# First stage of a two-block transformer kernel: the first gate row summed on GpSimd, the softplus chain moved to GpSimd

## The chip, the cores and the metric

The kernel runs on one core of one Trainium2 chip. Its engines are TensorE (PE in the profile, PEld for its weight loads), VectorE (DVE), ScalarE (ACT), GpSimd (POOL) and SyncE (SP), which here only issues DMAs. The metric is the device time of one execution in microseconds; the median of several runs is compared.

## What is computed

Two blocks run one after the other on 256 positions of width 1024, all in float32. The first block has two layers whose shifts, scales and gates are computed from a condition vector `c`. The part that matters here is the first half of its first layer, the RG-LRU mixer:

```python
c_act = jax.nn.silu(c)
mod = (c_act @ ada_w[i] + ada_b[i])[:, None, :]
sh_m, sc_m, gt_m, sh_f, sc_f, gt_f = jnp.split(mod, 6, axis=-1)
h = rmsnorm(x, norm_g[i, 0]) * (1.0 + sc_m) + sh_m
y = rglru_mixer(h, ...)          # first layer
x = x + gt_m * rmsnorm(y, norm_g[i, 1])
```

Inside the mixer, `log_a = -8 * r * softplus(-lam)` needs the softplus of one vector of 1024 values, and `r` and a second gate come from small block-diagonal products. After that come a scan along the positions, a GeLU gate branch of full width and the output projection. The row `gt_m * norm_g[0, 1]` is the gate row: 1024 values, the same for all positions, needed only when the output of the mixer is added to `x`. Everything behind that (the feed-forward part, the second layer, the second block of four layers) is the rest of the program, by far the most of the time, and the change does not touch it.

## The kernel before

The program is straight-line code, written with a framework that places the waits and picks the order of instructions on each engine: it follows the order of the program, but puts an instruction forward where the one ahead is not yet ready by its own reckoning. A DMA or an instruction that is pinned (`keep_in_program_order`) stays behind everything that was written before it on its engine. At run time each engine, and SP's queue of DMAs, works strictly in the order that was fixed. Tiles of one name share a fixed number of buffers (`bufs`); a load into a buffer waits on SP until the last reader of the buffer is done, and what stands behind it on SP waits too.

The weights come as chunks of 128x1024 (512 KB), tile `raw`, four buffers. Most are split into a high and a low half: ACT rounds the high half (line 369), VectorE subtracts it (line 370), and every product is made of three fast passes (lines 432 to 434 and 439 to 441) that read high and low halves.

The first stage runs as follows.

- `ada_init` loads `c` into all partitions and makes `cact`, twice the SiLU of `c`, in all partitions.
- `rg_x` (lines 552 to 589) normalises `x`, transposes it, and also transposes `cact` into `crep`: chunk `kk` of `crep` holds in row p the value of `cact` at position 128 kk + p, 128 times side by side. Then, for each of eight chunks, VectorE computes two entries per partition of shift and scale (line 503: a row of `ada` times `cact`, summed along the row; the loads go into `adar` or `adag`, two buffers each), ACT makes the modulated tile, and PE adds the products with the first weights (line 588) in eight PSUM banks.
- `rg` computes the softplus chain on VectorE (lines 794 to 812, tiles of 128x8 called `lam`): a polynomial in z. Then the convolution over four positions (ACT line 814, VectorE line 816), and a loop over four groups with the small gate products (PE line 833), tanh and exponentials on ACT (lines 836 to 847) and three products on VectorE (lines 845, 846, 849). After it come the scan (lines 857, 859) and eight chunks of the gate branch (`up`, lines 439 to 441; GeLU, line 867; line 868; the split of the result, lines 444 and 445). In between, `bg` puts further rows of `ada` for later stages into VectorE's stream (line 503 again, pinned).
- `gate0` is a generator that is advanced twice in each of the four groups. Each step loads 128 rows of the gate's weights (`adag`, 128x1024, line 604, pinned on SP) and multiplies them on PE with `crep[:, kk, :]` as the stationary matrix (line 606): all 128 output rows are the same sum over the 128 partitions, added up over the eight steps in two PSUM banks of tag `y`. Its end adds twice the bias with a one-row matmul (line 609) and writes `row0`, half the sum times the norm's weight (line 610).
- `out_proj` (lines 432 to 434) multiplies the result with the output weights, position half 0 first, then half 1. `turn` takes a finished half, multiplies it with the gate row (line 647), normalises (GpSimd lines 525, 416, 417 compute the reciprocal root for 128 rows), adds it to `x` and prepares the next stage's input.

PSUM has eight banks here, four of tag `y` and four of tag `u`. GpSimd has only the reciprocal roots and a few fills.

Of the kernel before, what the change touches and what calls it, by code (L numbers as in the profile page):

```python
# [8 lines left out]
F32 = mybir.dt.float32  # L9
# [458 lines left out]
class Block1:  # L468
# [84 lines left out]
    def rg_x(self):  # L553
# [12 lines left out]
        self.crep = self.R.tile([128, 8, 128], F32, name="crep", tag="crep", bufs=1)  # L566
        for q in range(0, 8, 4):
            p = k.bank("u", 4, (128, 4, 128))
            for j in range(4):
                nc.tensor.transpose(p[:, j, :], self.cact[:, (q + j) * 128:(q + j + 1) * 128], k.ident)  # L570
            self.ACT.copy(out=self.crep[:, q:q + 4, :], in_=p)
# [19 lines left out]
    def gate0(self):  # L591

        k, Q, R, nc = self.k, self.Q, self.R, self.nc
        two = R.tile([1, 128], F32, name="two", tag="two", bufs=1)
        self.V.memset(two, 2.0)
        b = Q.tile([1, D], F32, name="gb0", tag="xn", bufs=2)
        k.tc.keep_in_program_order(nc.sync.dma_start(out=b, in_=self.a["gateb"][0:1]))
        self.row0 = Q.tile([128, D], F32, name="grow", tag="grow", bufs=1)
        k.tc.keep_in_program_order(nc.sync.dma_start(out=self.row0, in_=self.a["gateb"][1].partition_broadcast(128)))
        p = [k.bank("y", 4) for _ in range(2)]  # L600
        half = [slice(n * 512, n * 512 + 512) for n in range(2)]
        for kk in range(8):
            w = R.tile([128, D], F32, name="adag", tag="adag", bufs=2)
            k.tc.keep_in_program_order(nc.sync.dma_start(out=w, in_=self.a["adag"][kk]))
            for n in range(2):
                nc.tensor.matmul(p[n], self.crep[:, kk, :], w[:, half[n]], start=kk == 0, stop=False)
            yield
        for n in range(2):
            nc.tensor.matmul(p[n], two, b[:, half[n]], start=False, stop=True)
            self.V.scalar_tensor_tensor(out=self.row0[:, half[n]], in0=p[n], scalar=0.5, in1=self.row0[:, half[n]], op0=OP.mult, op1=OP.mult)  # L610

    def gate_row(self, i, w):

        if (i, w) == (0, 0):
            return self.row0
# [169 lines left out]
    def rg(self):  # L785
        k, R, V, ACT = self.k, self.R, self.V, self.ACT
        x, ub = self.rg_x()
        n2 = lambda nm, w=512, b=2, dt=F32: R.tile([128, w], dt, name=nm, tag=f"r_{nm}", bufs=b)

        lam = self.col("rg_lambda", 0, 8)  # L790
        ab, e, z, sp = (k.small(f"lam{q}", 8) for q in range(4))
        ACT.activation(out=ab, in_=lam, func=AF.Abs)
        ACT.activation(out=e, in_=ab, func=AF.Exp, scale=-1.0)
        V.tensor_scalar(out=z, in0=e, scalar1=2.0, scalar2=None, op0=OP.add)
        V.reciprocal(out=z, in_=z)
        V.tensor_tensor(out=z, in0=z, in1=e, op=OP.mult)
        z2, acc = k.small("lam4", 8), k.small("lam5", 8)
        V.tensor_tensor(out=z2, in0=z, in1=z, op=OP.mult)
        V.memset(acc, 2.0 / 19)
        for d in range(17, 0, -2):  # L800
            V.tensor_tensor(out=acc, in0=acc, in1=z2, op=OP.mult)
            V.tensor_scalar(out=acc, in0=acc, scalar1=2.0 / d, scalar2=None, op0=OP.add)
        V.tensor_tensor(out=acc, in0=acc, in1=z, op=OP.mult)
        V.tensor_scalar(out=sp, in0=lam, scalar1=-1.0, scalar2=0.0, op0=OP.mult, op1=OP.max)
        V.tensor_tensor(out=sp, in0=sp, in1=acc, op=OP.add)
        sp2, sp4 = k.small("sp2", 8), k.small("sp4", 8)
        V.tensor_scalar(out=sp2, in0=sp, scalar1=2.0, scalar2=None, op0=OP.mult)
        V.tensor_scalar(out=sp4, in0=sp, scalar1=-4.0, scalar2=None, op0=OP.mult)
        hb = k.small("hb", 16)
        V.tensor_scalar(out=hb, in0=self.col("rg_ba", 0, 16), scalar1=0.5, scalar2=None, op0=OP.mult)  # L810
# [742 lines left out]
```

## Time and profile before

| | |
|---|---|
| median of three runs | 2728.43 us (2728.37 to 2731.88) |
| the profiled execution | 2730.44 us, span 2728.6 us |
| PE busy | 2664.6 us, 98% of the span |
| DVE busy | 1905.7 us, 70% |
| ACT busy | 1410.7 us, 52% |
| POOL busy | 77.4 us, 3% |
| moved by DMA | 514.38 MB, mean 189 GB/s |

The span is from the first to the last instruction on the core; the execution's time is 1.8 us longer. The profile gives, for each engine, its instructions in order of time with the idle time ahead of each and what ended that idle time. Busy shares over the whole span say little about the first stage, which is short and mixes several limits; it is read from stretches of 10 us and from the order of time. An fp32 matmul appears as two records. One fp32 record of 512 columns takes some 0.44 us from start to start. PE's granted clock is full for nearly the whole span.

### The profile page before, as it was taken

The numbers are of one execution on the slowest core, as the hardware profiler recorded it, in microseconds if no ns is written. First come the engines' busy times: TensorE is split into PE (matmuls) and PEld (weight loads), VectorE is DVE, ScalarE is ACT, GpSimd is POOL, SyncE is SP. The second block draws the span as 40 slices with busy tenths as digits, with TensorE's granted clock in tenths as the row PEclk, the third lists the DMA queues.
The fourth block names the chain that finished last, engine by engine and source line by source line (L and its number), as shares of the span: only waits on it lengthen the run. The fifth ranks groups of instructions, "written<-read, shape, count | busy, mean of one in ns | idle before, by whom it ended". The sixth has DMA issues, their size and how long they took to land.

```text
span 2728.6 us, 44400 instructions
## 1 busy us (share of the span) xinstructions
PE 2664.6 (98%) x16744; PEld 2360.5 (87%) x16744; DVE 1905.7 (70%) x3780; ACT 1410.7 (52%) x2848; POOL 77.4 (3%) x115
## 2 busy tenths in 40 slices
PE   7899999999999999999999999999999999999998
PEld 5689877898899779989988899899889989977898
DVE  6889889877656776575565755756775575685755
ACT  4665654655444655444455544544754454455542
POOL 0000000000000000000000000000000000000000
PEclk9999999999999999999999999999999999999999
DMA  8868674665655537656654565664455565453652
GB/s 316 293 239 300 220 247 158 216 201 167 209 186 166 155 113 225 185 180 199 184 172 123 181 185 170 214 185 148 149 170 186 170 209 186 155 181 114 208 185 93
DMA packets 141080, 514.38 MB, mean 189 GB/s; under 512 B 16177, under 2 KB 16561, under 8 KB 139330
## 3 DMA queue, kind: packets, MB, share of 16 engines
q1 hardware_dynamic: 140866, 511.56, 57.9%
q8 instruction: 131, 2.15, 0.3%
q14 instruction: 83, 0.68, 0.1%
HBM read 510.44 MB, written 1.05 MB: 187 GB/s over the span
## 4 chain that ended last, share of the span: by engine, by line
PE 85%; issue 6%; DVE 4%; ACT 2%; DMA 1%; POOL 1%; DVEq 0%; POOLq 0%; SPq 0%; ACTq 0%
PE u L439 12%; PE u L440 12%; PE u L441 12%; PE y L434 11%; PE y L432 11%; PE y L433 11%; PE u L432 3%; PE u L433 3%; PE u L434 3%; DVE lo L370 2%; PE u L1234 2%; PE u L463 1%; DMA raw<-w 1%; PE u L1228 1%; PE u L1211 1%
## 5 line engine op out<-in xcount | busy, mean ns | idle before, releaser
L370 DVE TENSOR_TENSOR lo<-raw,hi 128x512 fp32r<-128x512 f32 (+4 forms) x1501 | 1081.4, 747 | 557.6 <-ACT hi L369 546.7
L369 ACT CAST hi<-raw 128x512 fp32r<-128x512 f32 (+4 forms) x1501 | 953.3, 667 | 796.4 <-issue 447.4
L439 PE MATMUL u<-hThi,hi 128*128 128x256 f32 x3016 | 855.2, 284 | 2.0 <-ACT hi L369 1.4
L441 PE MATMUL u<-hThi,lo 128*128 128x256 f32 x3016 | 852.6, 283 | 0.5 <-DVE lo L370 0.5
L440 PE MATMUL u<-hTlo,hi 128*128 128x256 f32 x3016 | 852.9, 283 | 0.0
L439 PEld LDWEIGHTS u<-hThi,hi 128*128 128x128 f32 x3016 | 576.9, 191 | 6.7 <-ACT hi L369 1.6
L440 PEld LDWEIGHTS u<-hTlo,hi 128*128 128x128 f32 x3016 | 577.2, 191 | 4.6 <-issue 1.0
L441 PEld LDWEIGHTS u<-hThi,lo 128*128 128x128 f32 x3016 | 576.9, 191 | 1.1 <-DVE lo L370 1.0
L432 PE MATMUL y<-hi,hT 128*128 128x512 f32 x704 | 278.9, 396 | 0.0
L433 PE MATMUL y<-lo,hT 128*128 128x512 f32 x704 | 278.3, 395 | 0.0
L434 PE MATMUL y<-hi,hT 128*128 128x512 f32 x704 | 278.2, 395 | 0.0
L432 PE MATMUL y<-hi,hThi 128*128 128x512 f32 (+6 forms) x504 | 192.1, 382 | 3.5 <-ACT hThi L444 3.3
L433 PE MATMUL y<-lo,hThi 128*128 128x512 f32 (+6 forms) x504 | 187.8, 373 | 0.1
L434 PE MATMUL y<-hi,hTlo 128*128 128x512 f32 (+6 forms) x504 | 186.4, 373 | 0.2 <-DVE hTlo L445 0.2
L434 PEld LDWEIGHTS y<-hi,hT 128*128 128x128 f32 x704 | 132.3, 188 | 31.9
L432 PEld LDWEIGHTS y<-hi,hT 128*128 128x128 f32 x704 | 132.4, 188 | 29.2
L433 PEld LDWEIGHTS y<-lo,hT 128*128 128x128 f32 x704 | 132.2, 188 | 28.9
L432 PE MATMUL u<-hi,hThi 128*128 128x512 f32 x320 | 127.5, 400 | 5.4 <-ACT hThi L444 5.4
L444 ACT CAST hT<-th 128x256 fp32r<-128x256 f32 x144 | 58.3, 405 | 130.2 <-DVE th L1100 130.2
L433 PE MATMUL u<-lo,hThi 128*128 128x512 f32 x320 | 125.6, 394 | 0.0
L434 PE MATMUL u<-hi,hTlo 128*128 128x512 f32 x320 | 123.3, 393 | 0.0
L432 PEld LDWEIGHTS y<-hi,hThi 128*128 128x128 f32 x504 | 96.3, 191 | 19.4 <-ACT hThi L444 5.2
(303 smaller groups left out, 3192.9 us busy)
## 6 DMA issues: line engine op xcount, KB each, us to landing
raw<-w SPq DMA_DIRECT2D x823, 512.0 KB, 3.7
adar<-ada SPq DMA_DIRECT2D x80, 512.0 KB, 4.8
gb<-lngb SPq DMA_DIRECT2D x12, 1024.0 KB, 4.6
adag<-ada SPq DMA_DIRECT2D x8, 512.0 KB, 5.8
adag<-adag SPq DMA_DIRECT2D x8, 512.0 KB, 4.5
raw<-w SPq DMA_DIRECT2D x8, 384.0 KB, 3.0
raw<-w SPq DMA_DIRECT2D x5, 480.0 KB, 3.5
raw<-w SPq DMA_DIRECT2D x4, 396.0 KB, 3.0
```

What stands on the lines that cost most here:

```text
L369: nc.scalar.copy(out=hi[:, a:b], in_=r[:, a:b])
L370: nc.vector.tensor_tensor(out=lo[:, a:b], in0=r[:, a:b], in1=hi[:, a:b].bitcast(F32), op=OP.subtract)
L432: mm(out, xhi, w[0], start=start, stop=False)
L433: mm(out, xhi, w[1], start=False, stop=False)
L434: mm(out, xlo, w[0], start=False, stop=stop)
L439: mm(out, whi, xhi, start=start, stop=False)
L440: mm(out, whi, xlo, start=False, stop=False)
L441: mm(out, wlo, xhi, start=False, stop=stop)
L444: self.nc.scalar.copy(out=hi, in_=src)
L463: self.nc.tensor.transpose(p[:, k * 128:k * 128 + 128], x[:, (h + k) * 128:(h + k + 1) * 128], self.ident)
L1211: nc.tensor.matmul(scores[e], qh(e), kh(e), start=True, stop=True)
L1234: nc.tensor.matmul(op[:, e, :], pTs[e // 2][:, e % 2, j, :], v[j][:, e, :], start=j == 0, stop=j == t)
```

## The change

The eight chunks of the gate's weights no longer go to PE. `crep` is replaced by `ccol`, one column per chunk (128x8 in all). GpSimd multiplies each chunk with its column and adds it to a sum tile `gsum` (128x1024); the first partition of the sum also takes twice the bias. The sum over partitions is then made by two fp32 matmuls with a matrix of ones, in `gate_row`, which is called after the output projection of half 0 has been written; their banks have tag `u`. The loads of bias, norm row and chunks are no longer pinned on SP. The softplus chain runs on GpSimd; the reciprocal becomes a power of -1 with an exponent tile.

```diff
--- before.py
+++ after.py
@@ -563,12 +563,12 @@
                     nc.tensor.transpose(p[:, q, t * 128:t * 128 + 128], xn[t][:, (kk + q) * 128:(kk + q + 1) * 128], k.ident)
             self.ACT.copy(out=xT[:, kk:kk + 2, :], in_=p)
 
-        self.crep = self.R.tile([128, 8, 128], F32, name="crep", tag="crep", bufs=1)
+        self.ccol = self.R.tile([128, 8], F32, name="ccol", tag="ccol", bufs=1)
         for q in range(0, 8, 4):
             p = k.bank("u", 4, (128, 4, 128))
             for j in range(4):
                 nc.tensor.transpose(p[:, j, :], self.cact[:, (q + j) * 128:(q + j + 1) * 128], k.ident)
-            self.ACT.copy(out=self.crep[:, q:q + 4, :], in_=p)
+            self.ACT.copy(out=self.ccol[:, q:q + 4], in_=p[:, :, 0])
         acc = [k.bank("y" if j < 4 else "u", 4) for j in range(8)]
         h = self.h_tiles()
         mod, dot = self.mod[0], self.dot[0]
@@ -591,27 +591,33 @@
     def gate0(self):
 
         k, Q, R, nc = self.k, self.Q, self.R, self.nc
-        two = R.tile([1, 128], F32, name="two", tag="two", bufs=1)
-        self.V.memset(two, 2.0)
+        G = nc.gpsimd
         b = Q.tile([1, D], F32, name="gb0", tag="xn", bufs=2)
-        k.tc.keep_in_program_order(nc.sync.dma_start(out=b, in_=self.a["gateb"][0:1]))
+        nc.sync.dma_start(out=b, in_=self.a["gateb"][0:1])
         self.row0 = Q.tile([128, D], F32, name="grow", tag="grow", bufs=1)
-        k.tc.keep_in_program_order(nc.sync.dma_start(out=self.row0, in_=self.a["gateb"][1].partition_broadcast(128)))
-        p = [k.bank("y", 4) for _ in range(2)]
-        half = [slice(n * 512, n * 512 + 512) for n in range(2)]
+        nc.sync.dma_start(out=self.row0, in_=self.a["gateb"][1].partition_broadcast(128))
+        s = self.gsum = R.tile([128, D], F32, name="gsum", tag="gsum", bufs=1)
         for kk in range(8):
             w = R.tile([128, D], F32, name="adag", tag="adag", bufs=2)
-            k.tc.keep_in_program_order(nc.sync.dma_start(out=w, in_=self.a["adag"][kk]))
+            nc.sync.dma_start(out=w, in_=self.a["adag"][kk])
+            c = self.ccol[:, kk:kk + 1]
+            if kk == 0:
+                G.tensor_scalar(out=s, in0=w, scalar1=c, scalar2=None, op0=OP.mult)
+                G.tensor_scalar(out=b, in0=b, scalar1=2.0, scalar2=None, op0=OP.mult)
+                G.tensor_tensor(out=s[0:1], in0=s[0:1], in1=b, op=OP.add)
+            else:
+                G.tensor_scalar(out=w, in0=w, scalar1=c, scalar2=None, op0=OP.mult)
+                G.tensor_tensor(out=s, in0=s, in1=w, op=OP.add)
+            yield
+
+    def gate_row(self, i, w):
+
+        if (i, w) == (0, 0):
             for n in range(2):
-                nc.tensor.matmul(p[n], self.crep[:, kk, :], w[:, half[n]], start=kk == 0, stop=False)
-            yield
-        for n in range(2):
-            nc.tensor.matmul(p[n], two, b[:, half[n]], start=False, stop=True)
-            self.V.scalar_tensor_tensor(out=self.row0[:, half[n]], in0=p[n], scalar=0.5, in1=self.row0[:, half[n]], op0=OP.mult, op1=OP.mult)
-
-    def gate_row(self, i, w):
-
-        if (i, w) == (0, 0):
+                h = slice(n * 512, n * 512 + 512)
+                p = self.k.bank("u", 4)
+                self.nc.tensor.matmul(p, self.ones, self.gsum[:, h], start=True, stop=True)
+                self.V.scalar_tensor_tensor(out=self.row0[:, h], in0=p, scalar=0.5, in1=self.row0[:, h], op0=OP.mult, op1=OP.mult)
             return self.row0
         k, Q = self.k, self.Q
         m = self.mods(i, 3 * w + 2)
@@ -785,29 +791,32 @@
     def rg(self):
         k, R, V, ACT = self.k, self.R, self.V, self.ACT
         x, ub = self.rg_x()
+        G = k.nc.gpsimd
         n2 = lambda nm, w=512, b=2, dt=F32: R.tile([128, w], dt, name=nm, tag=f"r_{nm}", bufs=b)
 
         lam = self.col("rg_lambda", 0, 8)
         ab, e, z, sp = (k.small(f"lam{q}", 8) for q in range(4))
+        self.inv = k.small("inv", 8)
+        G.memset(self.inv, -1.0)
         ACT.activation(out=ab, in_=lam, func=AF.Abs)
         ACT.activation(out=e, in_=ab, func=AF.Exp, scale=-1.0)
-        V.tensor_scalar(out=z, in0=e, scalar1=2.0, scalar2=None, op0=OP.add)
-        V.reciprocal(out=z, in_=z)
-        V.tensor_tensor(out=z, in0=z, in1=e, op=OP.mult)
+        G.tensor_scalar(out=z, in0=e, scalar1=2.0, scalar2=None, op0=OP.add)
+        G.tensor_tensor(out=z, in0=z, in1=self.inv, op=OP.pow)
+        G.tensor_tensor(out=z, in0=z, in1=e, op=OP.mult)
         z2, acc = k.small("lam4", 8), k.small("lam5", 8)
-        V.tensor_tensor(out=z2, in0=z, in1=z, op=OP.mult)
-        V.memset(acc, 2.0 / 19)
+        G.tensor_tensor(out=z2, in0=z, in1=z, op=OP.mult)
+        G.memset(acc, 2.0 / 19)
         for d in range(17, 0, -2):
-            V.tensor_tensor(out=acc, in0=acc, in1=z2, op=OP.mult)
-            V.tensor_scalar(out=acc, in0=acc, scalar1=2.0 / d, scalar2=None, op0=OP.add)
-        V.tensor_tensor(out=acc, in0=acc, in1=z, op=OP.mult)
-        V.tensor_scalar(out=sp, in0=lam, scalar1=-1.0, scalar2=0.0, op0=OP.mult, op1=OP.max)
-        V.tensor_tensor(out=sp, in0=sp, in1=acc, op=OP.add)
+            G.tensor_tensor(out=acc, in0=acc, in1=z2, op=OP.mult)
+            G.tensor_scalar(out=acc, in0=acc, scalar1=2.0 / d, scalar2=None, op0=OP.add)
+        G.tensor_tensor(out=acc, in0=acc, in1=z, op=OP.mult)
+        G.tensor_scalar(out=sp, in0=lam, scalar1=-1.0, scalar2=0.0, op0=OP.mult, op1=OP.max)
+        G.tensor_tensor(out=sp, in0=sp, in1=acc, op=OP.add)
         sp2, sp4 = k.small("sp2", 8), k.small("sp4", 8)
-        V.tensor_scalar(out=sp2, in0=sp, scalar1=2.0, scalar2=None, op0=OP.mult)
-        V.tensor_scalar(out=sp4, in0=sp, scalar1=-4.0, scalar2=None, op0=OP.mult)
+        G.tensor_scalar(out=sp2, in0=sp, scalar1=2.0, scalar2=None, op0=OP.mult)
+        G.tensor_scalar(out=sp4, in0=sp, scalar1=-4.0, scalar2=None, op0=OP.mult)
         hb = k.small("hb", 16)
-        V.tensor_scalar(out=hb, in0=self.col("rg_ba", 0, 16), scalar1=0.5, scalar2=None, op0=OP.mult)
+        G.tensor_scalar(out=hb, in0=self.col("rg_ba", 0, 16), scalar1=0.5, scalar2=None, op0=OP.mult)
         xc = R.tile([128, 8, 256], F32, name="xc", tag="big0", bufs=1)
         for j in range(8):
             u = ub[j]
```

## Rows read from the trace of the kernel before

**Rows 1.** The page, part 1: busy us (share of the span) and instructions.

```profile
PE 2664.6 (98%) x16744; PEld 2360.5 (87%) x16744; DVE 1905.7 (70%) x3780; ACT 1410.7 (52%) x2848; POOL 77.4 (3%) x115
```

**Rows 2.** Stretches: length, then busy us and instructions per engine, PE clock, DMA.

```profile
70.00:80.00 10.00, 4.80 (x16) 3.09 (x16) 6.64 (x11) 8.56 (x16) 0.00 (x0) 0.87 0.87 313
80.00:90.00 10.00, 10.00 (x66) 8.29 (x65) 10.00 (x16) 8.04 (x11) 0.00 (x0) 0.95 0.93 342
```

**Rows 3.** PE in order: start, us, line, tiles, count, [idle before <-releaser].

```profile
50.66 3.66 PE L606 MATMUL y<-adag,crep 128*128 128x512 f32 x8
...
58.84 3.60 PE L606 MATMUL y<-adag,crep 128*128 128x512 f32 x8
...
78.00 2.93 PE L606 MATMUL y<-adag,crep 128*128 128x512 f32 x3 [5.20 <-DMA adag<-adag]
...
82.56 0.69 PE L439 MATMUL u<-hThi,hi 128*128 128x256 f32 x1
...
94.15 1.98 PE L609 MATMUL y<-gb,two 1*128 1x512 f32 x4
...
```

**Rows 4.** VectorE in order of time, 48 to 96 us.

```profile
53.19 4.75 DVE L816 SCALAR_TENSOR_TENSOR xc<-u,cols,xc 128x255 f32<-128x255 f32 x12
...
67.27 0.69 DVE L849 SCALAR_TENSOR_TENSOR xc<-wx,xc 128x512 f32<-128x512 f32 x1 [2.71 <-ACT wx L836]
...
76.70 1.23 DVE L503 SCALAR_TENSOR_TENSOR adar<-adar,cact 128x1024 f32<-128x1024 f32 x1 [3.32 <-DMA adar<-ada]
...
79.06 1.22 DVE L370 TENSOR_TENSOR lo<-raw,hi 128x1024 fp32r<-128x1024 f32 x1
...
94.58 1.21 DVE L370 TENSOR_TENSOR lo<-raw,hi 128x1024 fp32r<-128x1024 f32 x1
```

**Rows 5.** ACT in order of time, at 63 us.

```profile
63.45 0.63 ACT L847 ACTIVATE d<-d 128x512 f32<-128x512 f32 x1 [2.62 <-DVE wa L846]
```

**Rows 6.** VectorE and PE in order of time, 114 to 135 us.

```profile
119.21 1.23 DVE L370 TENSOR_TENSOR lo<-raw,hi 128x1024 fp32r<-128x1024 f32 x1 [0.40 <-ACT hi L369]
...
122.92 0.68 DVE L647 TENSOR_TENSOR yg<-y,grow 128x512 f32<-128x512 f32 x1
...
119.23 0.50 PE L432 MATMUL y<-hi,xchi 128*128 128x512 f32 x1 [0.41 <-ACT hi L369]
...
128.42 0.50 PE L433 MATMUL y<-lo,xchi 128*128 128x512 f32 x1 [0.76 <-DVE lo L370]
```

**Rows 7.** GpSimd's groups by shape: count | busy us, mean ns | idle before.

```profile
L525 POOL TENSOR_SCALAR mss<-ss 128x1 f32<-128x1 f32 x14 | 11.3, 808 | 539.4 <-ACT pj L646 504.6 <-ACT pj L654 22.8 <-DVE mod L514 12.0
...
L925 POOL MEMSET AT<- 128x1024 f32 x1 | 1.0, 951 | 3.6 <-PE y L434 3.6
L925 POOL MEMSET AT<- 128x512 f32 x1 | 0.5, 521 | 0.0
...
L416 POOL TENSOR_SCALAR ms<-ss 128x1 f32<-128x1 f32 x2 | 0.4, 190 | 5.1 <-ACT junk L536 5.1
```

**Rows 8.** GpSimd in order of time, at 342 us.

```profile
342.35 2.43 POOL L525 TENSOR_SCALAR mss<-ss 128x1 f32<-128x1 f32 x1
```

**Rows 9.** VectorE in order of time beside it.

```profile
342.20 1.21 DVE L370 TENSOR_TENSOR lo<-raw,hi 128x1024 fp32r<-128x1024 f32 x1
343.33 1.28 DVE L445 TENSOR_TENSOR hTlo<-hf,hThi 128x512 fp32r<-128x512 f32 x2
344.53 1.28 DVE L647 TENSOR_TENSOR yg<-y,grow 128x512 f32<-128x512 f32 x2
```

**Rows 10.** SP's queue in order of time: start, us, line, load, count.

```profile
44.66 1.67 SPq L604 DMA_DIRECT2D adag<-adag  x2
...
71.48 6.81 SPq L501 DMA_DIRECT2D adar<-ada  x2
```

**Rows 11.** The tile adag: time from a load's issue to its landing.

```profile
DMA to landing us min/median/max: 3.4/5.7/9.2
```

**Rows 12.** ACT in order of time, at 17 us.

```profile
17.36 0.60 ACT L548 ACTIVATE hf<-xnT,mod,A 128x256 f32<-128x256 f32 x1 [0.48 <-DVE lam L801]
```

More of the change, by code (lines that the diff above doesn't have):

```diff
@@ L607, in gate0 @@
             yield
-        for n in range(2):
-            nc.tensor.matmul(p[n], two, b[:, half[n]], start=False, stop=True)
-            self.V.scalar_tensor_tensor(out=self.row0[:, half[n]], in0=p[n], scalar=0.5, in1=self.row0[:, half[n]], op0=OP.mult, op1=OP.mult)
     def gate_row(self, i, w):
         if (i, w) == (0, 0):
+            for n in range(2):
+                h = slice(n * 512, n * 512 + 512)
+                p = self.k.bank("u", 4)
+                self.nc.tensor.matmul(p, self.ones, self.gsum[:, h], start=True, stop=True)
+                self.V.scalar_tensor_tensor(out=self.row0[:, h], in0=p, scalar=0.5, in1=self.row0[:, h], op0=OP.mult, op1=OP.mult)
```

## The prediction

> **What bounds the kernel now.** I read the page's engine shares first: PE is busy for 98% of the span [rows 1], so a microsecond that PE loses or wins in the first stage stays in the time to the end. Then the busy time in stretches of 10 us, because the change touches only the first 135 us: there the picture is another one. From 80 us on VectorE is busy for the whole of each stretch, and in 70 to 80 us PE stands still for half [rows 2]. Third, the instructions of each engine in order of time, to see which one waits for which.
>
> PE's timeline shows what the removed matmuls cost where they stand [rows 3]. The 16 fp32 matmuls appear as 32 records of line 606, eight of them in 3.6 us, so some 14 us in all; the two small ones of line 609, four records, take 2.0 us. But PE has to wait anyway. The first eight (from 50.66 us) lie beside the convolution of VectorE. The second eight (58.84 to 62.3 us) lie before products whose reader, ACT, is held: its row at 63.45 us waits for VectorE's line 846, and the tanh of those products comes only behind it [rows 5]. The third group begins with 5.20 us of waiting for a weight, and the gate branch's products start behind it at 82.56 us. They need the low half of a weight that VectorE begins at 79.06 and ends near 80.3 us. The last group ends at 96.1 us, just when VectorE has the next low half ready (94.58 + 1.21 = 95.8 us) [rows 4].
>
> So VectorE sets the pace from 60 to 119 us. Its gaps there are 2.71 us at 67.27 and 3.32 us at 76.70 us, 6.0 us together [rows 4]; after 76.70 us there is none of note until 119.21 us [rows 6].
>
> **The change part by part.**
>
> *TensorE's matmuls go.* By the above the first, second and last blocks are covered by VectorE or ACT. Of the third, PE could begin the gate products near 80.3 instead of 82.6 us, but it would only meet VectorE's next low halves sooner. I cost this edit at nothing. What hides it is VectorE's work; if VectorE came earlier, the removal would begin to pay.
>
> *The softplus chain moves to GpSimd.* 29 small VectorE instructions leave the first 25 us. Ahead of the first modulated tile they cost a little: ACT's row at 17.36 us waits 0.48 us, last for one of them [rows 12]. I take -0.5 us, between 0 (the weights of the next step are awaited anyway) and -1.0, twice that wait. On GpSimd the chain has until the gate tanhs behind the convolution, and is hidden there.
>
> *Eight weighted sums come to GpSimd.* No row shows GpSimd on a tile of that size with an input, so I bound it. Writing 128x1024 takes 0.95 us and 128x512 0.52 us, 0.84 ns per column; a one-column tensor-scalar takes 0.19 us [rows 7]. A one-input instruction is then 0.19 + 1024 x 0.84 ns = 1.05 us (estimate). The two-input add lies between one pass, 1.05 us, and three passes (two reads, one write), 2.75 us; I take two, 1.9 us, since only its second input is new against the one-input row. A chunk is then 2.95 us, between 2.1 and 3.8. [...]
>
> When does it run? The first chunk's DMA is issued at 44.66 us, when VectorE has released the buffer [rows 10], and lands 5.7 us later by the median [rows 11]: 50.4 us. Chunk 0 with the bias row (1.05 + 1.9) ends at 53.3, chunk 1 at 56.3, chunk 2 near 60 us. Until 57.9 us VectorE runs the convolution, whose first input is in PSUM [rows 4]. Five chunks are left, 14.75 us (10.5 to 19).
>
> Do they run beside VectorE? The trace has a row for that. GpSimd's one-column sum at 342.35 us takes 2.43 us and ends only after VectorE's two-input subtractions, which run until 344.61 us; the next VectorE row, with one input in PSUM, does not hold it [rows 8, 9]. The 14 sums of that line average 0.81 us, although a one-column tensor-scalar can take 0.19 us [rows 7]. So a GpSimd instruction that reads SBUF makes no progress while VectorE reads two SBUF operands, which nearly every VectorE instruction between 60 and 119 us does. Two streams that exclude each other add up: either VectorE waits, or GpSimd is put off past 119 us and the gate row, which VectorE's line 647 wants at 122.92 us [rows 6], is late by about as much. Either way 14.75 us have to fit into gaps of 6.0 us, which leaves +8.7 us (4.5 to 13). The rows show only GpSimd waiting, so the lower end for this term is below nothing as well, if VectorE never waits and the sums still end in time: then the gaps stay open to a gain (rival 1).
>
> [...]
>
> *Given back.* From 116 to 131 us PE waits four times for a high or low half, 2.3 us in all (the first and the last of the four stand in [rows 6]). High halves that wait for transfers would have landed if everything is 8.7 us late: -2.3 us (0 to -2.3).
>
> *The gate row's new place.* Two matmuls with the ones matrix, 2.0 us by the row of the two small ones, and line 610's two products on VectorE now come when the sum is ready. If PE reaches them inside VectorE's shadow they cost nothing, at the end of the output projection up to 2.0. I take +0.8.
>
> *DMA order.* The ten loads of the gate are no longer pinned on SP. A load waits on SP until its buffer is free, and everything behind it waits too: in the old kernel the pair issued at 71.48 us spends 6.81 us on the queue [rows 10]. Now it is GpSimd that frees the chunk buffers. I cost this at nothing in the sum (-2 to +8), and keep it for the rivals. ACT's smaller copy of the column saves time in a wait, nothing.
>
> Sum: -0.5 + 8.7 - 2.3 + 0.8 = +6.7 us on the profiled execution's 2730.4 us; that one is 2 us over the median of 2728.4, so the same sum on the median is 2735.
>
> **Rivals.**
>
> 1. *GpSimd fits beside VectorE, no gain.* VectorE always wins, GpSimd uses gaps and ends before 122 us. Then PE's relief meets VectorE's unchanged pace: between -2 and +2, near 2728. For it: the waiting rows all show GpSimd as the loser. Against: 14.75 us do not fit 6.0 us of gaps.
>
> 2. *Faster.* If the loads' freed order brings the transfer that VectorE awaits at 76.70 us early, and ACT takes the tanh before line 847's copy once PE's products come early, both gaps close: -0.5 - 3.3 - 2.7 = -6.5 us, 2722. It decides at the point where the five chunks cost VectorE less than about 1 us. For it: SP did stand behind pinned loads. Against: VectorE is full after that.
>
> 3. *The queues jam.* A chunk's load that waits for GpSimd stands on SP ahead of weights and ada rows, or PE reaches the ones matmul before the sum is complete; everything behind on SP or PE then waits for GpSimd's remaining chunks. Three chunks of 2.95 us on top of the forecast: +15.5 us, 2744. For it: GpSimd is the engine the order counts on and the trace shows it held. Against: when PE and VectorE stop, GpSimd runs free.
>
> That the change doesn't do what it says can be ruled out for its matmuls: they are no longer in the program.
>
> **How the numbers follow.** Forecast 0.49, rival 1 0.20, rival 2 0.16, rival 3 0.15. 0.2% is 5.5 us, about what a measurement of this kernel can tell from no change. The forecast's own range, 2731 to 2741, lies two thirds above 2734 (0.33 slower, 0.16 same). Slower: 0.33 + 0.15 = 0.48; same: 0.16 + 0.20 = 0.36; faster 0.16. The range from 2722 to 2744 takes in rival 1, about half of rival 2 and half of rival 3.
>
> **What would show it.** After the change VectorE's two-input rows between 60 and 125 us should be stretched over their old 0.68 and 1.22 us, or GpSimd's add rows should be far over 1.9 us; PE should wait more often for low halves; the gate row should be written after 110 us. If the add rows are near 1.2 us, or VectorE's rows keep their length and GpSimd is done by 90 us, the forecast is wrong toward rival 1 or 2. A chunk load that waits long on SP, with VectorE then waiting for ada rows, is rival 3.

## The result and the profile after

The changed kernel takes 2695.12 us (median of four runs, 2692.28 to 2697.15), the kernel before 2728.67 us beside it. The ratio is 0.987, 95% interval 0.986 to 0.989: 33.5 us faster. The forecast was 2735.0 us, range 2722 to 2744, so the sign is wrong and the time lies outside the range. The profiled execution of the changed kernel took 2695.8 us, its span is 2693.9 us.

The page of the changed kernel, part 1 (busy us, share of the span, instructions) and two groups of part 5 (busy us, mean ns of one, idle time before them). Part 1 answers to [rows 1].

```profile
PE 2606.5 (97%) x16712; PEld 2304.6 (86%) x16712; DVE 1910.6 (71%) x3750; ACT 1410.6 (52%) x2848; POOL 146.2 (5%) x162
...
L439 PE MATMUL u<-hThi,hi 128*128 128x256 f32 x3016 | 838.7, 278 | 15.9 <-ACT hi L369 15.5
L441 PE MATMUL u<-hThi,lo 128*128 128x256 f32 x3016 | 836.1, 277 | 6.9 <-DVE lo L370 6.9
```

The same groups on the page of the kernel before:

```profile
L439 PE MATMUL u<-hThi,hi 128*128 128x256 f32 x3016 | 855.2, 284 | 2.0 <-ACT hi L369 1.4
L441 PE MATMUL u<-hThi,lo 128*128 128x256 f32 x3016 | 852.6, 283 | 0.5 <-DVE lo L370 0.5
```

TensorE is busy 58 us less, though only 32 records of the first stage left it, some 15 us by the rows of eight in [rows 3]. The rest lies in products that the diff does not touch: each of the 9048 products of 128x256 in lines 439 to 441 is about 6 ns shorter, 50 us in the three groups together. The idle time ahead of them is longer instead (15.9 and 6.9 us against 2.0 and 0.5). So there are two effects of opposite sign, and they have to be read apart.

**First effect: the spacing of the products, in the whole kernel.** TensorE in order of time at 300 us (start, us, line, tiles). The kernel before:

```profile
299.98 0.28 PE L439 MATMUL u<-hThi,hi 128*128 128x256 f32 x1
...
300.70 0.28 PE L439 MATMUL u<-hThi,hi 128*128 128x256 f32 x1
```

The changed kernel:

```profile
299.92 0.28 PE L439 MATMUL u<-hThi,hi 128*128 128x256 f32 x1
...
300.61 0.28 PE L439 MATMUL u<-hThi,hi 128*128 128x256 f32 x1
```

Six products from start to start: 0.72 us before, 0.69 us after. Over all neighbours in these lines less than 0.4 us apart (some 8940 in each trace) the mean spacing is 120.1 ns before and 114.3 ns after, the median 120 and 113. Multiplied by 9048, 5.8 ns are 52 us. From 295 to 305 us the granted clock is 1.00 in both.

**Second effect: the first stage is longer.** A landmark outside the change is the first product of the next stage (line 432 with `hThi`; the numbers are read as above). Before:

```profile
142.83 0.39 PE L432 MATMUL u<-hi,hThi 128*128 128x512 f32 x1
```

After:

```profile
157.83 0.39 PE L432 MATMUL u<-hi,hThi 128*128 128x512 f32 x1
```

The stage loses 15.0 us; -52 and +15 make -37, against -34.7 us of span; the remaining 2 us are not traced. What does the stage lose its 15 us to? GpSimd in order of time in the changed kernel (lines 609 and 610 are the product and the add of one chunk), which answers to the estimates that rest on [rows 7]:

```profile
58.09 2.85 POOL L609 TENSOR_SCALAR adag<-adag,ccol 128x1024 f32<-128x1024 f32 x1
61.02 2.35 POOL L610 TENSOR_TENSOR gsum<-gsum,adag 128x1024 f32<-128x1024 f32 x1
...
84.11 3.97 POOL L609 TENSOR_SCALAR adag<-adag,ccol 128x1024 f32<-128x1024 f32 x1 [0.35 <-DMA adag<-adag]
88.17 3.40 POOL L610 TENSOR_TENSOR gsum<-gsum,adag 128x1024 f32<-128x1024 f32 x1
91.55 4.34 POOL L609 TENSOR_SCALAR adag<-adag,ccol 128x1024 f32<-128x1024 f32 x1
95.97 2.64 POOL L610 TENSOR_TENSOR gsum<-gsum,adag 128x1024 f32<-128x1024 f32 x1
```

A chunk takes 5.2 us undisturbed and up to 7.4 us beside VectorE; the last sum ends at 98.6 us. VectorE in the same stretch, answering to [rows 4]:

```profile
61.82 2.10 DVE L858 SCALAR_TENSOR_TENSOR xc<-wx,xc 128x512 f32<-128x512 f32 x1 [4.37 <-ACT wx L845]
...
75.48 2.27 DVE L503 SCALAR_TENSOR_TENSOR adar<-adar,cact 128x1024 f32<-128x1024 f32 x1 [3.87 <-DMA adar<-ada]
...
88.14 1.22 DVE L503 SCALAR_TENSOR_TENSOR adar<-adar,cact 128x1024 f32<-128x1024 f32 x1
...
89.28 3.37 DVE L503 SCALAR_TENSOR_TENSOR adar<-adar,cact 128x1024 f32<-128x1024 f32 x1
...
94.63 4.53 DVE L868 TENSOR_TENSOR_SCAN xc<-d,xc 128x256 f32<-128x256 f32 x4
```

Line 503 takes 1.22 us or 3.37 us with the same shape, line 858 0.69 us before (there line 849) and 2.10 here, the four scans 2.43 and 4.53. Added up, the stretched rows from 61 to 100 us (four of line 858, four of line 503, one group each of 866 and 868) are 12.1 us longer than their undisturbed kind. VectorE's idle time between the convolution and 100 us is 10.4 us against 8.5 before; together that is 14 us, near the stage's 15. Both sides are held: GpSimd's add goes from 2.35 us up to 3.40, and VectorE's rows hold their wait inside them.

The delay reaches TensorE by two ways. The first is SP's queue, in order of time (start, us on the queue), answering to [rows 10]:

```profile
50.46 8.02 SPq L602 DMA_DIRECT2D adag<-adag  x2
58.57 0.86 SPq L359 DMA_DIRECT2D raw<-w  x2
63.40 7.43 SPq L602 DMA_DIRECT2D adag<-adag  x2
```

The second is VectorE's and ACT's results. TensorE's rows with idle time ahead of them, answering to [rows 3]:

```profile
62.94 8.83 PE L842 MATMUL u<-xc,raw 128*128 128x256 f32 x32 [2.03 <-DMA raw<-w]
76.81 5.34 PE L842 MATMUL u<-xc,raw 128*128 128x256 f32 x16 [5.04 <-DMA raw<-w]
93.36 0.58 PE L439 MATMUL u<-hThi,hi 128*128 128x256 f32 x1 [11.21 <-ACT hi L369]
98.46 0.58 PE L439 MATMUL u<-hThi,hi 128*128 128x256 f32 x1 [4.31 <-ACT hi L369]
106.16 0.58 PE L441 MATMUL u<-hThi,lo 128*128 128x256 f32 x1 [6.90 <-DVE lo L370]
```

A chunk's loads stand 8.02 and 7.43 us on SP until GpSimd frees the buffers, and weights stand behind them. Stretches of the changed kernel (length, busy us and instructions of PE, PEld, DVE, ACT, POOL, then PE clock), answering to [rows 2]:

```profile
80.00:90.00 10.00, 2.15 (x10) 1.57 (x8) 9.25 (x12) 5.88 (x11) 9.49 (x4) 0.84 0.72 274
90.00:100.00 10.00, 1.59 (x4) 1.00 (x4) 10.00 (x10) 5.19 (x8) 8.53 (x3) 0.50 0.61 218
100.00:110.00 10.00, 3.84 (x18) 3.84 (x19) 9.52 (x14) 1.48 (x2) 0.00 (x0) 0.50 0.55 169
```

Where TensorE was busy 10.00 of 10 us before, in both of the first two stretches, it works 2.15, then 1.59. From 90 to 110 us its granted clock is 0.50; before the first product of this stretch it had stood idle for 11.21 us, until 93.36.

### The profile page after: what moved, and what is told of

It reads as the page before. It is cut to its first block, busy times and chain, and to the rows that moved or that the text cites. A ratio compares the mean times of both kernels' runs of the same rounds, so it can differ in the third digit from the quotient of the medians.

```text
span 2693.9 us, 44370 instructions
## 1 busy us (share of the span) xinstructions
PE 2606.5 (97%) x16712; PEld 2304.6 (86%) x16712; DVE 1910.6 (71%) x3750; ACT 1410.6 (52%) x2848; POOL 146.2 (5%) x162
## 3 DMA queue, kind: packets, MB, share of 16 engines
q8 instruction: 131, 2.15, 0.3%
HBM read 510.44 MB, written 1.05 MB: 190 GB/s over the span
## 4 chain that ended last, share of the span: by engine, by line
PE 81%; DVE 9%; DMA 4%; issue 3%; ACT 2%; POOL 1%; DVEq 0%; SPq 0%; POOLq 0%; ACTq 0%
PE u L441 11%; PE u L439 11%; PE u L440 11%; PE y L434 11%; PE y L432 11%; PE y L433 11%; DVE lo L370 3%; PE u L432 3%; DMA raw<-w 3%; PE u L433 3%; PE u L434 3%; PE u L1243 2%; PE u L463 1%; DVE adar L503 1%; PE u L1237 1%
## 5 line engine op out<-in xcount | busy, mean ns | idle before, releaser
L439 PE MATMUL u<-hThi,hi 128*128 128x256 f32 x3016 | 838.7, 278 | 15.9 <-ACT hi L369 15.5
L441 PE MATMUL u<-hThi,lo 128*128 128x256 f32 x3016 | 836.1, 277 | 6.9 <-DVE lo L370 6.9
L440 PE MATMUL u<-hTlo,hi 128*128 128x256 f32 x3016 | 836.2, 277 | 0.0
L439 PEld LDWEIGHTS u<-hThi,hi 128*128 128x128 f32 x3016 | 568.0, 188 | 21.1 <-ACT hi L369 16.2
L441 PEld LDWEIGHTS u<-hThi,lo 128*128 128x128 f32 x3016 | 567.6, 188 | 7.4 <-DVE lo L370 7.2
L440 PEld LDWEIGHTS u<-hTlo,hi 128*128 128x128 f32 x3016 | 568.0, 188 | 3.6
L414 POOL TENSOR_SCALAR rstd<-bnmv 128x1 f32<-128x1 f32 x24 | 12.4, 516 | 1933.9 <-DVE bnmv L1079 1933.9
```

What stands on the lines that cost most here:

```text
L439: mm(out, whi, xhi, start=start, stop=False)
L440: mm(out, whi, xlo, start=False, stop=False)
L441: mm(out, wlo, xhi, start=False, stop=stop)
```

## The experiments

The addresses of the program lead to the first theory. The new exponent tile `inv` (128x8, two buffers, 64 bytes per partition) stands in the permanent pool, and moves all tiles behind it by 64 bytes: the weight halves `hi` and `lo` too, while the activation halves `hThi` and `hTlo` stay. Before, each weight half starts a multiple of 128 bytes behind each activation half (41,728 = 326 x 128 from `hThi` to `hi`).

*Theory P (placement):* this shift is the gain, and the change proper costs time. *Rival S (stream):* the new order and pace of the first stage set a pattern in the following streams. For the loss, *theory X (exclusion):* GpSimd's and VectorE's instructions hold each other up; *rival Q (queue):* chunk loads that wait for GpSimd hold up what stands behind them on SP. (Where an edit adds a statement within a line, the diff shows that statement alone.)

**1. The shift alone.** Into the kernel before, ahead of the weight halves:

```diff
+        pad = k.P.tile([128, 16], F32, name="pad", tag="pad", bufs=1); k.nc.gpsimd.memset(pad, 0.0)
```

> The kernel before with one unused tile of 64 bytes per partition ahead of the weight halves (their addresses rise by 64 bytes, as the new exponent tile does in the changed kernel); the order on every engine is that of before. Theory P (placement): the spacing of the fast products of lines 439 to 441 falls from 120 to 113 ns without any part of the change, some 50 us: about 2677 us. Rival S (stream): the spacing belongs to the changed program, by its order or by the load taken off TensorE; then nothing moves: 2728 us and 120 ns.

Measured: 2679.38 us, ratio 0.981 (0.979 to 0.983). Mean spacing 114.3 ns, median 113. Its group on the page, to set beside those of before and after:

```profile
L439 PE MATMUL u<-hThi,hi 128*128 128x256 f32 x3016 | 837.4, 278 | 2.5 <-ACT hi L369 1.4
```

The order on TensorE, VectorE and ScalarE is that of the kernel before, so S falls. An unused tile gives 49 us, or 51 against the 2730.58 us of the kernel before in the runs beside it.

**2. The change without the shift.** In the changed kernel:

```diff
-        self.inv = k.small("inv", 8)
+        self.inv = R.tile([128, 8], F32, name="inv", tag="inv", bufs=1)
```

> The changed kernel, with the exponent tile taken from the stage's own pool, so that the weight halves lie at their addresses of before; the order on every engine is that of the changed kernel. Theory P: 120 ns again, and what is left is the change itself: the first stage 15 us longer than before, about 2744 us. Rival S: 2695 us and 113 ns as in the changed kernel.

Measured: 2745.93 us, ratio 1.0054 (1.0039 to 1.0069); spacing 120.6 ns; the landmark stands at 158.70 us. The change itself costs 15 us against the kernel before in the runs beside it (2730.58), 17 against 2728.67, and with the shift on both sides (2695.12 against 2679.38) 16 us.

**3 to 6. What about the place counts.** Experiment 3 puts the 64 bytes ahead of the activation halves, so that these and the weights move together; 4, 5 and 6 put 32, 128 and 96 bytes where experiment 1 has 64 (the pad's width in the diff above is 8, 32 and 24).

```diff
+            pad = self.P.tile([128, 16], F32, name="pad", tag="pad", bufs=1); self.nc.gpsimd.memset(pad, 0.0)
             self.hT = [self.P.tile([128, 8, 256], F32R, name=f"hT{p}") for p in ("hi", "lo")]
```

> The kernel before with the same 64 bytes ahead of the activations' halves (hT), so that both these and the weight halves rise by 64 bytes; weight addresses as in the changed kernel, distance to hT as before. Theory P1 (the distance between stationary weights and moving activations counts, modulo 128 bytes): 120 ns, 2728 us. Theory P2 (the weights' own address counts): 113 ns, about 2677 us. Rival S: 2728 us.

> The kernel before with 32 bytes ahead of the weight halves. If only an equal offset modulo 128 bytes is slow (P1 in its sharp form): 113 ns, about 2677 us. If the spacing depends on the distance gradually: between 113 and 120 ns, 2680 to 2725 us. If offsets count modulo 32 bytes only: 120 ns, 2728 us. Rival S: 2728 us.

> The kernel before with 128 bytes ahead of the weight halves. If the distance counts modulo 128 bytes: 120 ns and 2729 us, as without the tile. If any larger distance than before helps, or it counts modulo 256 or more: 113 to 117 ns, 2677 to 2722 us.

> The kernel before with 96 unused bytes ahead of the weight halves. If the spacing is a smooth curve of the distance with a period of 128 bytes and its lowest point near 64 bytes, this is the mirror of 32 bytes: about 117 ns and 2722 us. If 64 bytes is only a point on a longer slope, it is at or below 113 ns and 2680 us or less.

**7. Both.** 64 bytes at the place of experiment 3 and 64 at that of experiment 1: the weights move by 128, the distance grows by 64.

> The kernel before with 64 unused bytes per partition ahead of the activation halves (hT) and 64 more ahead of the weight halves (hi, lo): the activations stand at 96 instead of 32 bytes past a multiple of 128, the weights at 32 as in the kernel before, their distance is 64 bytes longer. Theory distance (what counts is how far the weights lie from the activations): spacing 113 ns as with 64 bytes ahead of the weights alone, about 2680 us. Rival own address of the weights: they stand at 32 past a multiple of 128 as in the kernel before, so 120 ns and about 2729 us.

Measured, with the spacing over all neighbours in lines 439 to 441 (ratios are to the kernel before run beside each, with medians of 2728.23 to 2730.58 us; the spacing is that of one profiled execution, with 32 bytes the slowest of its ten, 2727.18 us):

| added bytes ahead of activations / weights | distance grows by | spacing, mean (median) ns | time us | ratio, 95% interval |
|---|---|---|---|---|
| none (before) | 0 | 120.1 (120) | 2728.67 | 1 |
| 64 / 0 | 0 | 120.5 (120) | 2728.87 | 0.9996 (0.9987 to 1.0006) |
| 0 / 32 | 32 | 118.9 (117) | 2722.29 | 0.9967 (0.9958 to 0.9977) |
| 0 / 64 | 64 | 114.3 (113) | 2679.38 | 0.9812 (0.9794 to 0.9829) |
| 64 / 64 | 64 | 114.5 (113) | 2680.59 | 0.9820 (0.9802 to 0.9837) |
| 0 / 96 | 96 | 119.1 (119) | 2723.38 | 0.9984 (0.9974 to 0.9993) |
| 0 / 128 | 128 | 118.9 (119) | 2724.66 | 0.9987 (0.9978 to 0.9997) |

It is the distance of weights and activations, not the address of either: 64/0 changes nothing, 64/64 equals 0/64 although the weights then stand at the same place in 128 bytes as before. The smooth curve that I had expected is not there: only 64 bytes gives much; 32, 96 and 128 lie close together. With 128 bytes the spacing does not quite return to 120 ns, so the kernel does not show a plain period of 128 bytes. Other products lose at 32, 96 and 128 bytes: the 960 of 128x512 in lines 432 to 434 that write `u` and read `hThi` or `hTlo` go from a mean of 227.9 ns to 233.3, 233.5 and 232.7 (229.4 at 64), some 5 us in all.

**8. The products alone.** Behind the last stage of the kernel before come some 1500 products of the same shape, with the start of the stationary part moved by 0 to 192 bytes; in a second part VectorE subtracts and ACT copies 128x1024 beside them.

```diff
+        for c, j in C:
+            mm(p, s(hi, 16, c), m[:, j, :], start=j == 0, stop=j == 7)
```

> The kernel before, and behind its last stage some 1500 extra products of the same shape (128 x 256, fp32r, stationary part of a weight half, moving part of the activations) that measure the spacing by itself: stretches of 96 products whose stationary part starts 0, 32, 64, 96, 128 and 192 bytes later, first with every other engine and the DMAs silent, then (0, 64, 128 bytes) beside a stream of VectorE subtractions and ScalarE copies of 128 x 1024. The time of the whole means nothing. If the spacing comes from TensorE's own two reads (weights and activations), the stretches alone already differ: near 120 ns at 0, 117 at 32, 113 at 64, 119 at 96 and 128. If it needs the other engines' traffic, all are equal alone and differ only in the second part. If it is neither, all are equal in both parts.

TensorE in order of time; lines 422 to 436 are offsets of 0, 32, 64, 96, 128, 192, 0 and 64 bytes with all other engines silent, lines 451 to 457 are 0, 64, 128 and 64 bytes beside VectorE:

```profile
2764.99 11.68 PE L422 MATMUL u<-hThi,hip 128*128 128x256 f32 x96
2776.51 11.52 PE L424 MATMUL u<-hThi,hip 128*128 128x256 f32 x96
2787.86 11.47 PE L426 MATMUL u<-hThi,hip 128*128 128x256 f32 x96
2799.18 11.43 PE L428 MATMUL u<-hThi,hip 128*128 128x256 f32 x96
2810.44 11.68 PE L430 MATMUL u<-hThi,hip 128*128 128x256 f32 x96
2821.96 11.47 PE L432 MATMUL u<-hThi,hip 128*128 128x256 f32 x96
2833.27 11.68 PE L434 MATMUL u<-hThi,hip 128*128 128x256 f32 x96
2844.79 11.06 PE L436 MATMUL u<-hThi,hip 128*128 128x256 f32 x96
...
2868.41 11.68 PE L451 MATMUL y<-hThi,hiq 128*128 128x256 f32 x96
2879.93 11.47 PE L453 MATMUL y<-hThi,hiq 128*128 128x256 f32 x96
2891.24 11.56 PE L455 MATMUL y<-hThi,hiq 128*128 128x256 f32 x96
2902.63 11.04 PE L457 MATMUL y<-hThi,hiq 128*128 128x256 f32 x96
```

From the start of one row to the next, divided by 96: 120.0 ns at 0 bytes three times, 120.0 at 128 alone (118.6 beside VectorE), 117.3 to 118.2 at 32, 96 and 192. The granted clock is 1.00 from 2776.5 to 2787.7 us (32 bytes), from 2833.2 to 2855.5 (0 and 64), and beside VectorE from 2868.4 to 2879.7 (0) and 2902.6 to 2913.3 (64). So the effect needs no other engine: with the weights' start as the only difference the spacing changes while VectorE, ACT and GpSimd are silent and the DMAs are at a share of 0.01 or less (the first three of these stretches). But 64 bytes gave 117.9 and 113.5 ns alone, 117.8 and 113.3 beside VectorE (the second of each from the starts within the row), with the same addresses within each part. Something besides the distance decides between these two, and stays through a stretch; what it is these runs don't show. Both times the lower one came in the last stretch of its part, and the 192 bytes, 64 more than 128, gave 117.8, so the order of the stretches is not excluded. With silent engines the products thus show the step from 120.0 to some 118 ns at each of the offsets that are no multiple of 128 bytes (32, 64, 96 and 192), and the step to 113 in one of the two stretches at 64. In experiment 1 nearly all of the kernel settled at the lower one (88 of 93 runs of 96 products have a median of 113 or 114 ns).

**9. GpSimd only writes.** On the kernel of experiment 2, the products and adds become fills of about the same length (five of 128x1024 and a short one per chunk, 4.9 us; the first chunk, not shown, has two more). The kernel leaves out the gate row, which is zero.

```diff
-                G.tensor_scalar(out=w, in0=w, scalar1=c, scalar2=None, op0=OP.mult)
-                G.tensor_tensor(out=s, in0=s, in1=w, op=OP.add)
+                    G.memset(w[:, :1024], 0.0)
+                    G.memset(w[:, :1024], 0.0)
+                    G.memset(s[:, :1024], 0.0)
+                    G.memset(s[:, :1024], 0.0)
+                    G.memset(s[:, :1024], 0.0)
+                    G.memset(w[:, :64], 0.0)
```

> The changed kernel with the weight halves at their addresses of before, and GpSimd's two-input and scaling instructions on the chunks replaced by fills of the same buffers of about the same time (five of 128x1024 and one of 128x64 per chunk, 4.9 us by the 0.95 us of one fill), so that loads, queues and the order of the other engines stay; the gate row is left out of the computation (zero). Theory X (exclusion: a GpSimd instruction that reads holds VectorE and is held): VectorE's rows from 60 to 100 us return to 0.69 and 1.22 us, the 12 us by which they are stretched go, 2732 to 2736 us. Rival Q (queue: only the chunk loads that wait on SP cost time): 2742 to 2746 us, VectorE's rows shorter but with longer idle times.

Measured: 2730.91 us, ratio 1.0007 (0.9997 to 1.0016), 15.0 us under experiment 2 (13 by the two ratios); the landmark is at 144.61 us. VectorE in order of time:

```profile
66.08 0.69 DVE L866 SCALAR_TENSOR_TENSOR wa<-d 128x512 f32<-128x512 f32 x1
66.69 1.22 DVE L503 SCALAR_TENSOR_TENSOR adar<-adar,cact 128x1024 f32<-128x1024 f32 x1
```

GpSimd in the same stretch:

```profile
65.62 0.95 POOL L617 MEMSET adag<- 128x1024 f32 x1
66.52 0.94 POOL L616 MEMSET adag<- 128x1024 f32 x1
```

A fill keeps its 0.95 us and VectorE its 0.69 and 1.22 us. In these rows GpSimd's instructions that only write hold nobody up and are not held, unlike those that read. The total proves less, for two reasons. The chunk loads' time on SP fell as well, from 8.02 and 7.41 us to 1.46 each, so this run does not hold Q still. And GpSimd has less to do in this stretch: all 24 fills of the sum tile, which wait for no load, ran before 46 us. Stretches of this run (GpSimd is the fifth engine, then the PE clock):

```profile
60.00:70.00 10.00, 9.33 (x42) 7.83 (x40) 5.71 (x10) 8.53 (x20) 5.79 (x10) 0.96 0.75 270
70.00:80.00 10.00, 3.69 (x16) 2.96 (x16) 8.65 (x14) 7.84 (x18) 2.05 (x3) 0.89 0.79 290
80.00:90.00 10.00, 1.59 (x4) 1.01 (x4) 9.66 (x18) 6.47 (x9) 2.05 (x3) 0.50 0.85 325
90.00:100.00 10.00, 7.53 (x41) 7.53 (x42) 7.34 (x10) 2.81 (x4) 0.00 (x0) 0.59 0.76 275
```

From 60 to 90 us GpSimd is busy for 9.9 us, in experiment 2 for 29.6. So the run shows that GpSimd's reading work in this stretch costs the time; that it does so through VectorE's stretched rows is read from the rows. It also shows that the low clock is not the loss by itself: TensorE waits 9.96 us and then runs at 0.50 and 0.59 here too, and the landmark is 1.8 us later than in the kernel before.

**10. The chunk loads off SP.** On the kernel of experiment 2:

```diff
-            nc.sync.dma_start(out=w, in_=self.a["adag"][kk])
+            nc.gpsimd.dma_start(out=w, in_=self.a["adag"][kk])
```

> The changed kernel with the weight halves at their addresses of before, and the eight chunk loads issued by GpSimd itself, so that no load waits on SP for a chunk. Theory Q: the weights of the gate products come in time, 5 to 10 us less than with the loads on SP, 2736 to 2741 us. Theory X alone: VectorE's rows stay stretched and nothing is won, 2744 to 2748 us.

Measured: 2747.73 us, ratio 1.0074 (1.0057 to 1.0090). TensorE in order of time:

```profile
53.03 15.93 PE L842 MATMUL u<-xc,raw 128*128 128x256 f32 x64 [4.49 <-issue]
78.09 0.58 PE L439 MATMUL u<-hThi,hi 128*128 128x256 f32 x1 [9.13 <-ACT hi L369]
...
112.69 0.58 PE L439 MATMUL u<-hThi,hi 128*128 128x256 f32 x1 [12.92 <-ACT wx L876]
```

One of VectorE's rows:

```profile
85.61 3.41 DVE L503 SCALAR_TENSOR_TENSOR adar<-adar,cact 128x1024 f32<-128x1024 f32 x1
```

With SP free the 64 gate products run without a gap and the first `up` product comes at 78.09 instead of 92.58 us, but VectorE's rows are stretched as before, TensorE gives the lead back in a wait of 12.92 us, and the landmark is at 156.65 us. The queue is one way by which GpSimd's delay reaches TensorE; taking it away alone wins nothing. X stands, Q as the cause by itself falls. What the queue adds beside X is not measured: here each issue takes GpSimd 0.54 to 0.79 us, and VectorE's order is another, with low halves of line 370 ahead of the scans.

**11. The chain alone.** Only the softplus chain moves to GpSimd, with the `inv` tile and its shift; the gate sums stay on TensorE.

> Only the softplus chain on GpSimd, with its exponent tile (weight halves 64 bytes higher, as in the changed kernel); the gate sums stay on TensorE. If the chain brings the small gain that I had put down (0 to -1 us on top of the placement): 2677 to 2680 us, as the kernel before with 64 bytes alone (2679). If GpSimd's small instructions hold VectorE in the first 25 us as well: 2681 us or more.

Measured: 2677.50 us, ratio 0.9814 (0.9799 to 0.9828), the landmark at 141.19 us (142.66 in experiment 1). It beats both kernels, by the shift: against experiment 1's 2679.38 the chain's own gain can't be told from nothing.

**12. A second shift.** On experiment 11, 32 unused bytes in front of the second block's tiles.

```diff
+        qp = Q.tile([128, 8], F32, name="qpad"); nc.gpsimd.memset(qp, 0.0)
         self.cmask = Q.tile([128, 256], F32, name="cmask")
```

> The kernel with only the softplus chain on GpSimd (2677.5 us) plus 32 unused bytes per partition in front of the second block's tiles, which moves its attention and feed-forward activations (hT of the down products) against the weight halves. These 2052 products of 512 columns are spaced 233 ns now. Theory distance holds for all products: their spacing changes by some ns, up to 5 ns each way, 2052 x 5 ns = 10 us at most, so 2667 to 2688 us. Rival: products of 512 columns with weights of their own are bound otherwise: within 2 us of 2677.5.

Measured: 2689.02 us, ratio 0.9856 (0.9838 to 0.9874), just outside what either theory gave. The down products (2112 in the trace) kept 233 ns; the products of 128x256 rose from 114.1 to 115.5 ns in the mean, some 13 us over 9048, though weights and activations did not move against each other and TensorE's order is the same. The rise comes by whole stretches: 31 of 93 runs of 96 products have a median of 117 or 118 ns, most of them behind 719 us, against 3 in experiment 11. These are the two levels of experiment 8; what chooses between them stays open.

## Why the prediction was wrong

**The step that failed is the sum's frame: it has terms for instructions, waits and queues, and none for the tiles that the change adds.** The exponent tile entered as part of the chain (-0.5 us) and was taken to cost its instructions only; every product behind the first stage kept its length from the profile of before, without a word on why it should. Experiments 1 and 2 put that missing term at -49 to -51 us, seven times the whole sum. No rival held it either: the faster one had -6.5 us and a mechanism (closed gaps) that did not occur. What experiment 8 measured with silent engines is 120.0 ns at equal places in 128 bytes, and 117.9 or 113.5 at 64 bytes; for what reason, no run here shows.

**What was forecast as +6.7 us is +15 to +17 us** (experiments 1 and 2), so the sign of the change proper was right and its size too small. By its terms:

- *The chain, -0.5.* In experiment 11, where the chain alone moves, the next stage's landmark comes 1.5 us earlier than in experiment 1. The total can't tell it from nothing.
- *A chunk of 2.95 us, between 2.1 and 3.8.* 5.2 us undisturbed. The one-input product was put at 1.05 us from fills and a one-column row; it takes 2.85, more than the two-input add (2.35, put at 1.9). A row that only writes (0.95 us, [rows 7]) was no measure for one that reads.
- *Five chunks left at 60 us.* GpSimd was in its third chunk by then; five adds started behind 66 us. Five chunks of 5.2 us are 26 us instead of 14.75, and with the forecast's own 6.0 us of gaps that would have been +20: above the +12.1 us that the stretched rows show. The gaps were wider than the 6.0 us of the sum: VectorE's idle time from the convolution to 100 us was 8.5 us before, with 2.44 us ahead of 60.38 that the sum left out, and is 10.4 us in the changed kernel, 4.37 and 3.87 of them in front of two rows.
- *Mutual exclusion.* Right, and stronger than the rows of before showed: VectorE is held as well, 3.37 us instead of 1.22, and GpSimd's add beside it takes 3.40 instead of 2.35. That GpSimd's reading is what matters agrees with the rows of experiment 9, where a fill keeps its 0.95 us and VectorE beside it its 0.69 and 1.22.
- *Given back, -2.3.* About right in kind: of the waits behind [rows 6] one of 0.76 us is left in the changed kernel's output projection, so 1.5 of 2.3 us came back.
- *The gate row's new place, +0.8.* TensorE's two matmuls take 1.02 us each, at 137.03 and 143.61, and VectorE reads the first half of the row at 142.10 us; no idle time stands ahead of those matmuls, and the sum was ready at 98.6. "The gate row after 110 us" held, but by its place in the program, not by GpSimd.
- *DMA order, nothing (-2 to +8).* The chunk loads did stand on SP (8.02 and 7.43 us), and TensorE waited 2.03 and 5.04 us for weights behind them. That is rival 3's mechanism, and its 2744 us lies 2 us from experiment 2's 2745.93. But experiment 10 takes the queue away and wins nothing, so it is not the loss by itself; its share is not measured.
- *TensorE's matmuls, nothing gained.* Right: what it no longer multiplies, it waits.

What was not in any term is the granted clock: behind TensorE's long wait its products run at a granted clock of 0.50 (from 90 to 110 us). No run separates that share, but in experiment 9 stretches at 0.50 and 0.59 cost little: the landmark is 1.8 us later than in the kernel before.

## What to carry to other kernels

Before pricing a change, look what its tiles move: a small permanent tile ahead of the weights can shift the spacing of thousands of untouched products behind it (here 64 bytes, 120.1 to 114.3 ns), and an unused tile of 64 bytes is a cheap experiment that beats this whole change. A one-input GpSimd instruction that reads SBUF is not cheap beside a VectorE that reads two SBUF operands: here 128x1024 took 2.85 us undisturbed and up to 4.34 beside it, and VectorE's line 503 3.37 us instead of 1.22. Price its length from a row that reads, and take the two lengths added, less the gaps, as the upper end (+20 us by that sum, 15 to 17 measured). When a stage gets longer and the total shorter, compare the mean duration of untouched groups first.

## What the runs showed of the hardware that I had not expected

- Products of 128x256 with a new weight load each run 120 ns apart at the kernel's own distance of weights and activations, a multiple of 128 bytes per partition; 113 to 114 ns with 64 bytes more, 117 to 119 with 32, 96 or 128. With all other engines silent it is 120.0 ns at 0 and 128 bytes, 117.3 to 118.2 at 32, 96 and 192, and at 64 bytes both 117.9 and 113.5 occur.
- The down products of 128x512, whose activations lie in a tile that moves with the weights, keep 233.3 to 233.5 ns in the mean in every one of the kernels of the table. Those that write `u` and read the activation halves do change, and by another pattern: 227.9 ns before, 233.3 with 32 bytes, 229.4 with 64.
- GpSimd's one-input product over 1024 columns takes 2.85 us, on 128 partitions as on one (the bias row, 1x1024), and is slower than its add of two inputs, 2.35 us.
- GpSimd's products of 128x8 in the softplus chain took 0.20 us or up to 1.26 us with the same shape; what decides was not tested. The whole chain lasted from 8.7 to 27 us and was still hidden.
